# New duration estimates in the driver that orders a hybrid layer's instructions

## The chip, the cores and the metric

The kernel runs on one core of a Trainium2 chip. The core has a matrix engine (TensorE, PE in the profile), three engines for elementwise work (VectorE or DVE, ScalarE or ACT, GpSimd or POOL) and a queue that issues transfers (SyncE, SP); each of them works through its own instructions strictly in the order in which the program lists them. The metric is the time of one execution on the device in microseconds, as the median of several runs.

## What is computed

One layer of a generator over 1024 latent tokens and 256 context tokens of width 1024, in single precision:

```python
pl = project(modulate(x, sh_x, sc_x), w_in)        # 1024 latent tokens, 11 streams
pc = project(modulate(ctx, sh_c, sc_c), w_in)      # 256 context tokens
s_f = gla_final_state(kc, vc, la_fc)               # states after the context
s_b = gla_final_state(rev(kc), rev(vc), rev(la_bc))
o_gla = bidir_gla(q, k, v, la_f, la_b, s_f, s_b)   # 4 heads, both directions
a1 = softmax(q1 @ [ck1, k1].T / 8); a2 = softmax(q2 @ [ck2, k2].T / 8)
o_diff = (a1 - lam * a2) @ [cv, dv]                # 8 heads, 1024 queries, 1280 keys
a = rms_norm(o_gla) * gla_gain * silu(gla_gate)
b = rms_norm(o_diff) * diff_gain * (1 - lam_init) * silu(diff_gate)
y = sigmoid(m_gla) * (a @ w_br_gla) + sigmoid(m_diff) * (b @ w_br_diff)
x = x + g_x * (y @ w_out)
```

Before this a small product makes shifts, scales and gates from the conditioning. Queries and keys of the attention are normalised and rotated by position.

## The kernel before

Every large product is made of three matmuls on 128x128 weights and up to 512 columns (`mm3`): each operand is held as a high part `hi` in a faster format and a remainder `lo`, and the products hi·hi, hi·lo and lo·hi are added up. The split itself is work for ScalarE or GpSimd (the copy `hi`) and VectorE or GpSimd (the subtraction `lo`).

The work has these stages, in the order of the span:

- **Prologue** (`prologue`, `consts`, `consts_late`): inputs are loaded and normalised, the conditioning's product is made, the tokens are transposed into the tiles `h`.
- **Projections** (`stream` in `phase_a`): fifteen jobs, each 512 columns of the input projection for all tokens. Their results go to PSUM tiles `mm`, through ScalarE, VectorE and GpSimd, and out to memory. This stream has the lowest priority among the tasks, 9, and fills what time TensorE has left beside other tasks.
- **Linear attention** (GLA, `gla_head`): four heads one after another, from the eighth job of the stream on. A head loads its tensors (tile `gk` and others), makes running sums, transposes keys (tile `gt`), carries a state along ten chunks backward and forward (`upd`: a matmul on TensorE, then one VectorE instruction that adds it to the decayed state `gsb` or `gsf`), computes the products inside chunks (`intra`: differences and products on VectorE, exponentials on ScalarE) and combines them in the tile `go`. Its buffers are single or double.
- **Change of buffers**: when GLA is done, its pools are closed and the pools of attention's operands opened (`to_gla` sets `ev_b2`); then keys `kk`, values `vv` and queries `aq` are loaded. When the projections are done too, PSUM is handed over (`to_b` sets `ev_b`), and attention may begin.
- **Differential attention** (`att_scores`, `att_max`, `att_exp`, `att_mix`, `att_tr`, `att_split`, `att_av`, `att_fin`): 64 steps, one for each of 8 heads and 8 tiles of 128 queries. A step makes two sets of scores (PSUM tiles `st` and `s2`, the latter shown as `s` in the profile), takes maxima on VectorE and exponentials on ScalarE, combines the two softmaxes on VectorE, transposes the result on TensorE (PSUM tiles `b`), copies it on ScalarE (tile `ac`), splits it on GpSimd (tiles `at`), and multiplies it with the values. Every second step ends in a normalisation (`att_fin`, tiles `b1k`).
- **Fill** (`fill`): the rest of the projections (12 blocks of 128 columns) and the two branch products are cut into half tiles of 24 matmuls, which run at priority 9 beside attention in one PSUM bank (`mb`), and later in the banks `mc`. The number of half tiles that may have started is bound to the number of attention steps by `PACE = 1.3`.
- **End** (`phase_c`): the last branch products and the output projection.

What sets the order is the class `Driver`. While the program is being built, all stages run as Python generators, and the driver keeps a clock of its own: `now` for TensorE, and for each other engine the time `free` at which it has finished what it was given. Each emitted instruction goes through `Driver.op` with an estimated cost. It starts at the latest of its engine's free time and the times at which its operands are ready; it ends after its cost; and its result is ready `LAT` later (0.24 us for PE, 0.15 us for the others). A generator yields the time at which it wishes to go on, or an event; the driver takes the due generator of the best priority, and where none is due moves `now` forward. Generators that yield such a time are taken up to 1.0 us earlier (`AHEAD`), those that name an engine when that engine has at most 1.0 us of work left (`SLACK`). The estimates do not alter any instruction: they decide at which place of its engine's list, and of the transfer queue, each one stands. The chip then works through these lists, with waits where data aren't there yet.

The costs are set in `Engine.emit`, in `Hybrid.mm` (line 317 is the matmul), in `Hybrid.tr` (a transpose, line 329) and for transfers in `Driver.dma`. The profile attributes every elementwise instruction to line 185, every matmul to line 317 and every transpose to line 329, since these are helpers; tiles tell them apart.

Of the kernel before, what the change touches and what calls it, by code (L numbers as in the profile page):

```python
# [10 lines left out]
F32R = mybir.dt.float32r  # L11
# [45 lines left out]
class Driver:  # L57
# [58 lines left out]
        return At(end)  # L116

    def dma(self, nbytes, dst, src):
        t = max(self.free["DGE"], self.now, self.ready.get(self.key(src), 0.0)) + 0.6
        self.free["DGE"] = t  # L120
        t = max(self.free["DMA"], t + 0.6) + nbytes / 360e3
        self.free["DMA"] = t
        t += 1.8
        k = self.key(dst)
        self.ready[k] = max(t, self.ready.get(k, 0.0))
        return At(t)
# [48 lines left out]
class Engine:  # L175
# [5 lines left out]
    def __getattr__(self, what):  # L181
        f = getattr(self.eng, what)

        def emit(out, *args, **kw):
            f(out, *args, **kw)  # L185
            isap = lambda x: hasattr(x, "free_size")
            ins = [x for x in list(args) + list(kw.values()) if isap(x)]
            outs = [out] + [kw[k] for k in ("accum_out",) if k in kw]
            n = out.free_size()
            if what == "tensor_reduce":  # L190
                n = args[0].free_size()
            scalars = sum(1 for x in ins if x.free_size() == 1 and n > 1)
            psum = any(x.space == PSUM for x in ins)
            if self.name == "ACT":
                c = 0.06 + 0.000833 * n + 0.093 * scalars + (0.0 if psum else 0.04)
            elif self.name == "DVE":
                fast = what in ("tensor_scalar", "tensor_copy") and not psum
                c = 0.07 + n / 960 * (0.5 if fast else 2.0 if "scan" in what else 8.0 if what == "reciprocal" else 1.0)
            elif ALU.pow in args:
                c = 0.3 + 0.165 * n  # L200
            elif what == "tensor_tensor":
                c = 0.15 + 0.0021 * n
            else:
                c = 0.16 + 0.00083 * n + 0.083 * scalars
            return self.d.op(self.name, c, outs, ins)

        return emit
# [6 lines left out]
class Hybrid:  # L214
# [101 lines left out]
    def mm(self, out, lhsT, rhs, start, stop):  # L316
        self.nc.tensor.matmul(out, lhsT, rhs, start=start, stop=stop)  # L317
        n = rhs.free_size()
        c = (max(n, 256) if rhs.dtype == F32R else 2 * max(2 * n, 256)) / 2400
        return self.d.op("PE", c, [out], [lhsT, rhs])  # L320

    def mm3(self, out, sh, sl, mh, ml, first, last):
# [1588 lines left out]
```

## Time and profile before

| | |
|---|---|
| median of 3 runs | 1772.32 us (1772.30, 1772.32, 1776.98) |
| profiled execution | 1774.69 us, span 1773.0 us |
| instructions | 25057 |
| matmuls and transposes on TensorE | 8633, busy 96% of the span |
| VectorE, ScalarE, GpSimd busy | 60%, 43%, 41% |
| transfers | 260 MB, mean 147 GB/s |
| TensorE clock granted | 0.99 |

A matmul's duration in the profile runs from its start to a modelled end and overlaps with the next one; the distance from one start to the next is what a matmul costs in a sequence. In the timeline and in the chain, neighbouring instructions of one kind are merged into a row with their count ("x24"). A timeline row shows the start, the time taken, the engine, the line, the operation, the tile written and the tiles read, and in brackets the idle time ahead of it and what ended that. A row of the waits shows who waited for whom, the total in microseconds, the number of waits, and the longest. Times are counted from the start of the span.

### The profile page before, as it was taken

To read this page: it belongs to the slowest core of one execution; us is meant where nothing else is said; L and a number is where in the kernel's file an instruction comes from. 1 tells how busy PE (TensorE), PEld (TensorE's weight loads), DVE (VectorE), ACT (ScalarE), POOL (GpSimd) and SP (SyncE) were. 2 spreads that over 40 slices of the span, in tenths; PEclk is the share of its full clock that TensorE was granted. 3 is DMA by queue.
4 is the path that set the end of the run, shared out by engine and by line. 5 is a ranking of instruction groups with operands and counts; after the bars stand their busy time and mean duration, and the time that the engine had idled before them with its cause. 6 is when DMAs were issued, how large, how long until landed. Compare 5 with 4: busy or idle time off the path is not lost.

```text
span 1773.0 us, 25057 instructions
## 1 busy us (share of the span) xinstructions
PE 1703.7 (96%) x8633; PEld 1400.7 (79%) x8633; DVE 1057.8 (60%) x1895; ACT 761.9 (43%) x1759; POOL 735.6 (41%) x914
## 2 busy tenths in 40 slices
PE   8799999999999999999999999999999898999999
PEld 3688868888888888788788788788887787888887
DVE  4524332625564767878861987777877678525532
ACT  5536442212233444443442666666665555522200
POOL 1500000412323435545530477777876776731000
PEclk9899999999999999999999999999999999999999
DMA  7522452343653645546447245345447652268522
GB/s 275 174 88 101 154 173 89 108 142 122 182 181 117 190 141 144 178 137 176 137 134 193 71 121 145 96 125 128 116 114 234 184 150 93 81 200 301 185 101 84
DMA packets 245991, 259.97 MB, mean 147 GB/s; under 512 B 21948, under 2 KB 177508, under 8 KB 245864
## 3 DMA queue, kind: packets, MB, share of 16 engines
q1 hardware_dynamic: 245864, 258.37, 47.4%
q8 instruction: 68, 1.11, 0.3%
q14 instruction: 59, 0.48, 0.1%
HBM read 171.79 MB, written 86.52 MB: 146 GB/s over the span
## 4 chain that ended last, share of the span: by engine, by line
PE 77%; DVE 12%; DMA 3%; ACT 3%; issue 2%; POOL 1%; SPq 1%; ACTq 0%; DVEq 0%; POOLq 0%
PE mm L317 37%; PE mc L317 12%; PE mb L317 7%; DVE sm L185 6%; PE b L317 5%; PE s L317 4%; PE b L329 3%; PE go L317 2%; PE st L317 2%; PE tp L329 2%; PE gs L317 2%; PE gt L317 1%; DVE e L185 1%; DVE b1k L185 1%; DVE gd L185 1%
## 5 line engine op out<-in xcount | busy, mean ns | idle before, releaser
L317 PE MATMUL mm<-w,h 128*128 128x512 f32 x2304 | 570.5, 399 | 0.5 <-ACT w L185 0.3
L317 PEld LDWEIGHTS mm<-w,h 128*128 128x128 f32 x2304 | 425.7, 188 | 86.5 <-ACT w L185 0.7
L185 POOL TENSOR_TENSOR at<-ac,at 128x512 fp32r<-128x512 f32 (+1 forms) x192 | 237.6, 1237 | 16.0
L317 PE MATMUL mb<-h,wt 128*128 128x512 f32 x792 | 213.7, 406 | 5.5 <-DVE ft L185 5.3
L185 POOL TENSOR_SCALAR at<-ac 128x512 fp32r<-128x512 f32 (+1 forms) x192 | 136.4, 710 | 168.1 <-ACT ac L185 167.1
L185 POOL TENSOR_SCALAR sm<-sm 128x1 f32<-128x1 f32 (+1 forms) x78 | 18.6, 239 | 444.7 <-DVE sm L185 348.5
L185 DVE TENSOR_TENSOR w<-raw,w 128x512 fp32r<-128x512 f32 x136 | 97.8, 737 | 119.6 <-ACT w L185 117.3
L317 PEld LDWEIGHTS mb<-h,wt 128*128 128x128 f32 x792 | 140.1, 189 | 31.5 <-DVE ft L185 6.0
L185 ACT ACTIVATE p<-mm 128x512 f32<-128x512 f32 (+1 forms) x116 | 67.4, 588 | 218.1 <-PE mm L317 200.2
L185 ACT ACTIVATE ac<-b 128x512 f32<-128x512 f32 (+1 forms) x213 | 107.4, 511 | 122.2 <-PE b L329 102.6
L185 DVE TENSOR_REDUCE sm<-s 128x1 f32<-128x1024 f32 x128 | 155.6, 1216 | 2.8 <-PE s L317 1.6
L185 ACT ACTIVATE e<-s,sm 128x1024 f32<-128x1024 f32 x128 | 143.9, 1124 | 0.0
L317 PE MATMUL b<-at,vv 128*128 128x256 f32 x960 | 130.8, 290 | 9.6 <-ACT ac L185 7.1
L317 PE MATMUL mm<-h,w 128*128 128x512 f32 x576 | 138.6, 397 | 0.1
L317 PEld LDWEIGHTS b<-at,vv 128*128 128x128 f32 x960 | 123.4, 194 | 15.8 <-ACT ac L185 9.6
L317 PE MATMUL s<-kk,aq 128*128 128x512 f32 x512 | 132.7, 396 | 0.3 <-ACT p L185 0.3
L317 PEld LDWEIGHTS mm<-h,w 128*128 128x128 f32 x576 | 108.6, 191 | 24.8 <-DVE h L185 0.8
L185 POOL TENSOR_TENSOR sm<-sm,nhalf 128x1 f32<-128x1 f32 (+2 forms) x110 | 114.8, 1044 | 30.5 <-DVE sm L185 21.1
L185 DVE SCALAR_TENSOR_TENSOR e<-e,sm,e 128x1280 f32<-128x1280 f32 x64 | 103.8, 1622 | 0.1
L317 PEld LDWEIGHTS s<-kk,aq 128*128 128x128 f32 x512 | 90.9, 189 | 15.4 <-ACT p L185 0.5
L185 ACT ACTIVATE w<-raw 128x512 fp32r<-128x512 f32 x136 | 82.2, 626 | 40.3 <-PE mm L317 25.6
L329 PE MATMUL b<-ident,e 128*128 128x128 f32 x604 | 94.3, 278 | 5.0 <-ACT ac L185 4.5
(195 smaller groups left out, 2649.2 us busy)
## 6 DMA issues: line engine op xcount, KB each, us to landing
raw<-in_w_in SPq DMA_DIRECT2D x72, 512.0 KB, 4.6
aq<-d_qT SPq DMA_DIRECT2D x128, 128.0 KB, 4.1
d_kT<-pl SPq DMA_DIRECT2D x40, 256.0 KB, 2.3
d_dv<-pl SPq DMA_DIRECT2D x40, 256.0 KB, 2.3
gv<-d_v SPq DMA_DIRECT2D x40, 256.0 KB, 3.2
kk<-d_kT SPq DMA_DIRECT2D x32, 320.0 KB, 4.1
vv<-d_dv SPq DMA_DIRECT2D x16, 640.0 KB, 8.4
d_aT<-gpl SPq DMA_DIRECT2D x64, 128.0 KB, 1.9
```

Of the source, the lines that this page charges most:

```text
L185: f(out, *args, **kw)
L317: self.nc.tensor.matmul(out, lhsT, rhs, start=start, stop=stop)
L329: self.nc.tensor.transpose(out, src, self.ident[:n, :n])
```

## The change

Only the estimates change, in three places: transfers, elementwise instructions and matmuls. In the elementwise formulas n is the number of elements per partition; `scalars` counts operands of one element per partition (an accumulator output counted among them before), `psum` says that an input lies in PSUM, and `acc` that the instruction has an accumulator output.

```diff
     def dma(self, nbytes, dst, src):
-        t = max(self.free["DGE"], self.now, self.ready.get(self.key(src), 0.0)) + 0.6
+        t = max(self.free["DGE"], self.now, self.ready.get(self.key(src), 0.0)) + 0.45
         self.free["DGE"] = t
...
             scalars = sum(1 for x in ins if x.free_size() == 1 and n > 1)
             psum = any(x.space == PSUM for x in ins)
+            acc = "accum_out" in kw
+            scalars -= acc and n > 1
             if self.name == "ACT":
-                c = 0.06 + 0.000833 * n + 0.093 * scalars + (0.0 if psum else 0.04)
+                c = 0.2 + 0.000833 * n + 0.093 * scalars - (0.028 if psum else 0.0) + (0.21 if acc else 0.0)
             elif self.name == "DVE":
                 fast = what in ("tensor_scalar", "tensor_copy") and not psum
-                c = 0.07 + n / 960 * (0.5 if fast else 2.0 if "scan" in what else 8.0 if what == "reciprocal" else 1.0)
+                c = 0.16 + 0.055 * scalars + n * 0.00104 * (
+                    0.5 if fast else 2.0 if "scan" in what else 8.0 if what == "reciprocal" else 1.0)
             elif ALU.pow in args:
-                c = 0.3 + 0.165 * n
+                c = 0.4 + 0.155 * n
             elif what == "tensor_tensor":
-                c = 0.15 + 0.0021 * n
+                c = 0.18 + 0.00216 * n
             else:
-                c = 0.16 + 0.00083 * n + 0.083 * scalars
+                c = 0.19 + 0.00084 * n
             return self.d.op(self.name, c, outs, ins)
...
         self.nc.tensor.matmul(out, lhsT, rhs, start=start, stop=stop)
         n = rhs.free_size()
-        c = (max(n, 256) if rhs.dtype == F32R else 2 * max(2 * n, 256)) / 2400
+        c = 0.009 + max(n, 230) * 0.000428 if rhs.dtype == F32R else 0.006 + max(4 * n, 470) / 2400
         return self.d.op("PE", c, [out], [lhsT, rhs])
```

A transpose keeps its cost of 0.109 us, and `LAT`, `AHEAD`, `SLACK`, the priorities and `PACE` stay as they are.

## The prediction

> **What bounds the kernel now.** I read the page first, then busy time by stage, then the timelines of single engines, the chain and the waits. The page says that TensorE is the bound, so other engines matter only where they keep it waiting.
>
> ```profile
> span 1773.0 us, 25057 instructions
> PE 1703.7 (96%) x8633; PEld 1400.7 (79%) x8633; DVE 1057.8 (60%) x1895; ACT 761.9 (43%) x1759; POOL 735.6 (41%) x914
> PE 77%; DVE 12%; DMA 3%; ACT 3%; issue 2%; POOL 1%; SPq 1%; ACTq 0%; DVEq 0%; POOLq 0%
> ```
>
> The second view cuts the span where the work changes: prologue, projections alone, linear attention (GLA) beside projections, projections alone again, differential attention beside the fill, and the end. Its columns are width, then busy time with instruction counts per engine, clock, DMA share and GB/s.
>
> ```profile
> 0.00:90.00 90.00, 69.62 (x295) 42.12 (x296) 47.44 (x80) 47.96 (x87) 32.81 (x57) 0.91 0.65 223
> 90.00:480.00 390.00, 385.63 (x1769) 313.19 (x1768) 157.72 (x234) 136.51 (x210) 57.57 (x60) 1.00 0.39 125
> 480.00:936.00 456.00, 448.86 (x2204) 372.68 (x2204) 315.78 (x673) 182.91 (x475) 202.63 (x314) 1.00 0.51 155
> 936.00:968.50 32.50, 32.50 (x145) 26.90 (x144) 2.36 (x2) 5.16 (x8) 0.00 (x0) 1.00 0.97 235
> 968.50:1536.00 567.50, 535.24 (x3149) 454.51 (x3148) 443.83 (x772) 350.02 (x907) 404.76 (x442) 0.99 0.46 129
> 1536.00:1773.00 237.00, 231.86 (x1080) 191.32 (x1078) 90.63 (x135) 39.30 (x73) 37.80 (x42) 1.00 0.49 168
> ```
>
> TensorE is idle for 20.4 us in the prologue, 4.4 in the projections, 7.1 beside GLA, nothing from 936 to 968.5, 32.3 in attention and 5.1 at the end. The change adds and removes no instruction. It can only move work between these gaps, so attention's 32.3 us is the prize and the full stretch at 936 is what can be lost.
>
> **What the new figures say, against the trace.** The driver uses a cost for two things: when the engine is free again, and when the result is ready (the end plus LAT, 0.15 us, or 0.24 for PE). Here is ScalarE working without a gap.
>
> ```profile
> 1165.71 0.47 ACT L185 ACTIVATE e<-st,sm 128x256 f32<-128x256 f32 x1 [1.35 <-DVE sm L185]
> 1166.08 0.19 ACT L185 ACTIVATION_READ_ACCUMULATOR e<-st,sm 128x1 f32 x1
> 1166.17 1.11 ACT L185 ACTIVATE e<-s,sm 128x1024 f32<-128x1024 f32 x1
> 1167.17 0.20 ACT L185 ACTIVATION_READ_ACCUMULATOR e<-s,sm 128x1 f32 x1
> 1167.26 0.60 ACT L185 ACTIVATE ac<-b 128x512 f32<-128x512 f32 x1
> 1167.74 0.60 ACT L185 ACTIVATE ft<-mb 128x512 f32<-128x512 f32 x1
> ```
>
> From start to start the small exponential takes 0.46 us, the large one 1.09, the copy 0.48. The old formula gives 0.459, 1.099 and 0.4865: it is the distance between starts. The new one gives 0.688, 1.328 and 0.5985, which is the duration shown (0.60 for the copy) or the sum of an instruction's and its accumulator read's durations. VectorE shows the same.
>
> ```profile
> 1165.93 1.54 DVE L185 SCALAR_TENSOR_TENSOR e<-e,sm,e 128x1280 f32<-128x1280 f32 x1
> 1167.39 0.15 DVE L185 SCALAR_TENSOR_TENSOR sm<-sm,sm 128x2 f32<-128x2 f32 x1
> 1170.19 0.69 DVE L185 TENSOR_REDUCE sm<-st 128x2 f32<-128x512 f32 x1 [1.01 <-PE st L317]
> 1170.80 0.15 DVE L185 TENSOR_REDUCE sm<-sm 128x2 f32<-128x4 f32 x1
> ```
>
> Distances are 1.46 and 0.61, durations 1.54 and 0.69. The old figures are 1.403 and 0.603, the new 1.546 and 0.692. So the new costs take an engine as occupied for its whole latency, and LAT is then added to that: a copy's result was due 0.4865 + 0.15 = 0.64 us after its start, which is about right for a 0.60 us instruction, and is now due at 0.75. GpSimd hardly moves: the 512-wide subtraction goes from 1.225 to 1.286, against 1.337 here.
>
> ```profile
> L185 POOL TENSOR_TENSOR at<-ac,at 128x512 fp32r<-128x512 f32 x128 | 171.1, 1337 | 10.7
> 326.82 5.49 PE mm L317 x24
> ```
>
> TensorE goes the other way. The chain's piece of 24 matmuls takes 5.49 / 24 = 0.229 us each; the driver believed 512 / 2400 = 0.213 and will believe 0.228. So far its PE clock ran 7% fast, which gave every other engine 7% less time per matmul than it has: a margin that was hidden there. The new PE figure takes that margin away and the new ACT and DVE figures put a larger one in its place.
>
> The Trainium skill (Perfetto Trace Analysis, "Optimizing Scalar/DVE Operations") says that a ScalarE or VectorE instruction's profiled latency holds about twice the access overhead for which the engine is busy, because the write acknowledgement overlaps with the next instruction. The rows above agree (0.60 shown, 0.48 apart). By that rule the new occupancies are too long and the old ones right, and it speaks against this half of the change.
>
> **Linear attention: price of the longer estimates.** In this stage the driver puts as many projection matmuls (three at a time, 3 x 0.213 = 0.64 us, new 0.684) between two steps of GLA as it thinks the step takes. One step of the state recurrence is here:
>
> ```profile
> 650.28 0.59 PE L317 MATMUL gt<-gv,gkt 128*128 128x256 f32 x2
> 650.52 1.73 PE L317 MATMUL mm<-w,h 128*128 128x512 f32 x6
> 650.91 0.48 DVE L185 SCALAR_TENSOR_TENSOR gsb<-gsb,gsm,gt 128x256 f32<-128x256 f32 x1 [0.59 <-PE gt L317]
> ```
>
> After the state matmul the driver waited 0.24 + 0.337 + 0.15 = 0.727 us, and will wait 0.24 + 0.481 + 0.15 = 0.871. In units of three matmuls that is 1.14, then 1.27: 12% more. The key transposes' copy (0.273 to 0.385) goes from 1.04 to 1.13 units, 9% more. In the intra-chunk step (two 128-wide subtractions, an exponential, a product, 0.15 after each) it is 1.51 to 1.88 us, or 2.35 to 2.74 units, 16% more. About 12% more projection work is thus asked for between GLA steps. Not all of it comes: a wait of 1.14 or 1.27 units is two units either way, as the six matmuls of the row show, and GLA's own matmuls do not stretch. The bounds are 0 (all rounded away) and 12%; I take the middle, 6%.
>
> GLA runs from the first head's load at 480 to its last transposes at 934.4:
>
> ```profile
> 479.98 0.50 SPq L282 DMA_DIRECT2D gk<-d_k  x1
> 934.37 0.38 PE L329 MATMUL tp<-ident,gp 128*128 128x128 f32 x2
> 934.50 34.31 PE L317 MATMUL mm<-h,w 128*128 128x512 f32 x150
> 937.25 3.72 SPq L282 DMA_DIRECT2D kk<-d_kT  x6
> 941.01 8.26 SPq L282 DMA_DIRECT2D vv<-d_dv  x3
> 949.32 6.71 SPq L282 DMA_DIRECT2D aq<-d_qT  x8
> aq<-d_qT SPq DMA_DIRECT2D x128, 128.0 KB, 4.1
> 968.65 0.64 PE L317 MATMUL st<-kk,aq 128*128 128x256 f32 x4
> ```
>
> So 6% of 454 us is 27 us. What hides it is the block of 150 projection matmuls that is left when GLA ends, 34.2 us. But that block already hides something: keys, values and queries of attention are loaded only once GLA's buffers are closed, and go through one queue. The first pair's four query transfers are issued by about 949.32 + 6.71 / 2 = 952.7 and land 4.1 later, at 956.8, which is 22 us after GLA's end. Only 968.65 - 956.8 = 12 us are spare. Total projection work is fixed, so GLA may end 12 us later for nothing; every further microsecond leaves TensorE with neither projections nor loaded queries. Price: 27 - 12 = +15 us; bounds 0 and 54 - 12 = +42.
>
> **Attention: what it may give.** The waits there are for results that the driver thought ready:
>
> ```profile
> PE b L329 <- DVE b1k L185: 8.7, 10, 3.9
> PE b L317 <- ACT ac L185: 7.1, 5, 1.7
> PE mb L317 <- DVE ft L185: 5.3, 3, 2.9
> PE b L329 <- ACT ac L185: 4.5, 6, 1.9
> ```
>
> They are transposes and products placed too early behind ACT and DVE work. Longer estimates place them later, with fill matmuls before them. The ACT waits (11.6 us) are the ones whose estimate grows most (copy and LAT per 512-wide matmul: 0.6365 / 0.213 = 2.99, then 0.7485 / 0.228 = 3.28, 10% more). The products also wait for GpSimd's splitting, which in the same measure becomes shorter (1.375 / 0.213 = 6.46, then 1.436 / 0.228 = 6.30), so I count only half of the ACT waits and no other: -6 us. Bounds: 0, and -20 if nearly two thirds of the 32.3 us go. Should fewer fill matmuls be left afterwards, the end stage, idle for 5 us now, loses its cover; that is a rival below.
>
> **DMA and prologue.** The issue figure of 0.6 us becomes 0.45; the rows above have 0.50 for one key load and 0.84 for a query load. The estimate shifts issue by tenths, so I take 0. The prologue holds one long wait of a transpose for VectorE, which any reordering may lengthen or remove; bounds -10 and +10, taken as 0 since nothing in the formulas points either way.
>
> ```profile
> PE gt L329 <- DVE p L185: 10.7, 2, 10.1
> ```
>
> **Sum.** The profiled execution took 1774.69 us (span 1773.0 and 1.7 around it), 2.4 above the median of the three runs (1772.32; 1772.30 to 1776.98). 1774.7 + 15 - 6 + 0 = 1783.7; as a median 1783.7 - 2.4, about 1781.
>
> **The rivals.** (1) Attention gains and GLA stays under its cover. This ends faster. It decides where GLA's stretch is under 12 us, 2.7% of 454, so where whole units of three matmuls swallow most of the 12%. For it: the six-matmul row, and GLA's stage is nearly free of waits as it is. Against it: the intra-chunk step is longer than two units and has room to grow. Time: -10 of attention's 32.3 us (the ACT waits almost whole), 1772.3 - 10 = 1762; with the bound of -20, 1752.
> (2) The fill runs out. Attention has 64 query tiles and may use 40 half tiles of fill of 24 matmuls; these rows show how many ran there.
>
> ```profile
> L317 PE MATMUL mb<-h,wt 128*128 128x512 f32 x792 | 213.7, 406 | 5.5 <-DVE ft L185 5.3
> ```
>
> That is 792 / 24 = 33, so seven are left. If longer estimates open wider gaps, a rate over 40 / 33 = 1.21 times as high empties them early. A query tile without fill still needs VectorE's 443.83 / 64 = 6.9 us, against TensorE's own (535.24 - 33 x 24 x 0.229) / 64 = 5.5: 1.4 us idle each, 17 us for the last twelve. 1772.3 + 17 = 1789. Against it: a copy's wait grows by only 10%.
> (3) The order hardly changes or gains and losses cancel: 1772.
>
> **Chances and range.** Forecast (GLA outlasts its spare cover) 0.42; rival 1 0.36; rival 2 0.10; rival 3 0.12. Faster 0.36, same 0.12, slower 0.52, taking 0.3% or 5 us as the least that a measurement of this kernel tells from no change. Both signs are likely. The forecast's own range is 1775 to 1808, from GLA's +42 less attention's 6 at the top to a stretch just beyond its cover at the bottom. The range that holds 8 in 10 reaches down through most of rival 1: 1754 to 1808.
>
> **What would show it.** In the profile after, GLA's last transposes should come at about 960 instead of 934, the block of pure projection matmuls behind them should shrink from 150 to under 60, and the first score matmul should stand at about 983 with TensorE idle ahead of it, released by DMA `aq`. Attention's idle time should fall from 32 to about 26 us, with the waits on ACT `ac` shorter. Wrong: GLA ends before 947 and the first scores stay at 968; then the time is set by attention alone, and faster if its idle time falls below 27. Wrong too: `mb` matmuls well over 960, which means the fill ran out, or a change of over 5 us before 90 us.

## The result and the profile after

The change makes no difference that can be told: 1776.12 us median (1770.69 to 1778.61, 14 runs) against 1775.09 us before (14 runs); ratio 1.0003, 95% interval 0.9994 to 1.0012. The profiled execution took 1776.08 us with a span of 1774.4, 1.4 us over the span of before.

Under this equal sum the stages moved. These are the same cuts of busy time as before the change (width, then PE, PEld, DVE, ACT, POOL, clock, DMA share, GB/s).

```profile
0.00:90.00 90.00, 69.84 (x286) 41.67 (x287) 46.89 (x80) 48.20 (x87) 32.68 (x57) 0.91 0.63 220
480.00:936.00 456.00, 455.66 (x2239) 381.86 (x2239) 304.03 (x666) 181.43 (x470) 192.98 (x307) 1.00 0.50 156
936.00:968.50 32.50, 25.31 (x119) 20.77 (x118) 4.44 (x9) 7.04 (x15) 2.52 (x8) 0.94 0.64 159
968.50:1536.00 567.50, 533.24 (x3165) 456.38 (x3166) 438.12 (x773) 351.25 (x907) 397.15 (x446) 0.98 0.47 133
```

Beside linear attention TensorE's idle time fell from 7.1 us to 0.3. From 936 to 968.5, where it had none, it has 7.2. The timeline of TensorE after the change shows that hole, and the transfer queue's shows what fills it.

```profile
950.67 0.38 PE L332 MATMUL tp<-ident,gp 128*128 128x128 f32 x2
950.80 10.51 PE L320 MATMUL mm<-h,w 128*128 128x512 f32 x45
973.85 1.51 PE L320 MATMUL st<-kk,aq 128*128 128x256 f32 x4 [12.54 <-DMA aq<-d_qT]
```

```profile
481.38 0.51 SPq L285 DMA_DIRECT2D gk<-d_k  x1
952.45 3.71 SPq L285 DMA_DIRECT2D kk<-d_kT  x6
956.20 9.29 SPq L285 DMA_DIRECT2D vv<-d_dv  x3
965.54 7.73 SPq L285 DMA_DIRECT2D aq<-d_qT  x8
```

Linear attention runs from 481.38 to 950.67, 469.3 us instead of 454.4. 45 projection matmuls are left behind it instead of 150. They are done at 961.3, and TensorE waits 12.54 us for the queries, which stand in the queue behind six key loads and three value loads. The first scores come at 973.85 instead of 968.65, only 5.2 us later, because TensorE had lost less time beside linear attention.

The price of the wait does not end with it. These are the first eight large score matmuls, before and after the change, and the stretch after the change in which the latter ran.

```profile
969.55 2.11 PE L317 MATMUL s<-kk,aq 128*128 128x512 f32 x8 [0.26 <-ACT p L185]
975.16 3.37 PE L320 MATMUL s<-kk,aq 128*128 128x512 f32 x8
973.85:978.10 4.25, 4.25 (x11) 3.38 (x12) 1.68 (x2) 0.00 (x0) 0.00 (x0) 0.50 0.86 253
```

The granted clock fell to 0.50 during the wait, at 964.5, and stayed there until 978.1. So the first 4.25 us of attention ran at half speed, which is worth about 2 us (an estimate: half of 4.25). TensorE counts as busy in such a stretch, so the busy share does not show the loss.

From the first scores to the end of the span it takes 800.5 us instead of 804.4, though single profiles of one order differ by as much: the fourth experiment below has the order of before in attention (two of TensorE's 4224 instructions stand at other places) and takes 800.4. What TensorE waits for in the attention window has changed its kind:

```profile
PE b L332 <- ACT ac L185: 12.8, 15, 1.4
PE st L320 <- DMA aq<-d_qT: 12.5, 1, 12.5
PE b L332 <- DVE b1k L185: 10.1, 15, 1.4
PE b L320 <- ACT ac L185: 3.1, 3, 1.0
```

The products' waits for the copies `ac` fell from 7.1 us to 3.1, and the fill's waits for `ft` from 5.5 us (5.3 of them on VectorE) to 0.7; the transposes' waits for `ac` rose from 4.5 us to 12.8.

### The profile page after: what moved, and what is told of

Same layout as the page of the kernel before. It is cut to its first block, busy times and chain, and to the rows that moved or that the text cites. A ratio compares the mean times of both kernels' runs of the same rounds, so it can differ in the third digit from the quotient of the medians.

```text
span 1774.4 us, 25140 instructions
## 1 busy us (share of the span) xinstructions
PE 1700.1 (96%) x8633; PEld 1403.5 (79%) x8633; DVE 1037.6 (58%) x1895; ACT 762.2 (43%) x1759; POOL 716.2 (40%) x914
## 4 chain that ended last, share of the span: by engine, by line
PE 86%; DVE 4%; DMA 3%; POOL 2%; ACT 2%; issue 2%; SPq 1%; ACTq 0%; POOLq 0%; DVEq 0%
PE mm L320 40%; PE mc L320 12%; PE mb L320 8%; PE b L320 6%; PE s L320 5%; PE b L332 3%; PE go L320 3%; DVE sm L185 2%; POOL at L185 2%; PE gs L320 2%; PE gt L320 2%; PE st L320 2%; PE tp L332 2%; SPq L285 1%; DMA w<-in_w_ada 1%
## 5 line engine op out<-in xcount | busy, mean ns | idle before, releaser
L185 POOL TENSOR_TENSOR at<-ac,at 128x512 fp32r<-128x512 f32 (+1 forms) x192 | 221.9, 1156 | 16.0
L320 PE MATMUL mb<-h,wt 128*128 128x512 f32 x792 | 219.9, 407 | 1.2 <-ACT ft L185 0.7
L185 POOL TENSOR_SCALAR at<-ac 128x512 fp32r<-128x512 f32 (+1 forms) x192 | 145.2, 756 | 158.7 <-ACT ac L185 149.3
L320 PE MATMUL mm<-h,w 128*128 128x512 f32 x576 | 144.4, 403 | 2.0 <-DVE h L185 1.5
L320 PE MATMUL s<-kk,aq 128*128 128x512 f32 x512 | 137.7, 404 | 0.0
L332 PE MATMUL b<-ident,e 128*128 128x128 f32 x604 | 94.1, 275 | 23.5 <-ACT ac L185 12.8
L185 POOL TENSOR_TENSOR sm<-sm,nhalf 128x1 f32<-128x1 f32 (+2 forms) x110 | 108.2, 983 | 13.7 <-DVE sm L185 7.2
L332 PEld LDWEIGHTS b<-ident,e 128*128 128x128 f32 x604 | 71.7, 140 | 44.7 <-ACT ac L185 18.6
L185 ACT ACTIVATE e<-st,sm 128x256 f32<-128x256 f32 x128 | 60.7, 474 | 99.8 <-DVE sm L185 83.6
```

The costliest lines, as they stand in the source:

```text
L332: self.nc.tensor.transpose(out, src, self.ident[:n, :n])
```

## Experiments

Ratios are to the kernel before, run beside each on the same chip, with 95% intervals. A thousandth is 1.8 us.

**1. The matmul estimate alone.**

```diff
-        c = (max(n, 256) if rhs.dtype == F32R else 2 * max(2 * n, 256)) / 2400
+        c = 0.009 + max(n, 230) * 0.000428 if rhs.dtype == F32R else 0.006 + max(4 * n, 470) / 2400
```

> Only the matmul estimate is the new one (0.213 to 0.228 us for 512 columns); elementwise and transfer estimates are the old ones. Theory (the hidden margin of 7% is taken away, nothing is put in its place): linear attention ends earlier, with some 246 projection matmuls left behind its last transposes instead of 150, so at about 934 - 96 x 0.229 = 912 us; the query loads stay hidden; TensorE waits more often beside linear attention and in attention (its idle time there above 35 us instead of 32), and the time is 3 to 12 us longer than before. Rival (the true rate of TensorE is the useful part): idle time falls in attention and the time is 3 us or more shorter than before.

Measured: 1803.99 us, ratio 1.0173 (1.0156 to 1.0189), about 30 us slower, far more than expected. TensorE's timeline around the end of linear attention, then the queue's:

```profile
917.11 0.38 PE L329 MATMUL tp<-ident,gp 128*128 128x128 f32 x2
945.55 41.79 PE L317 MATMUL mm<-h,w 128*128 128x512 f32 x174 [11.68 <-ACT w L185]
987.18 0.64 PE L317 MATMUL st<-kk,aq 128*128 128x256 f32 x4
```

```profile
922.03 3.05 SPq L282 DMA_DIRECT2D kk<-d_kT  x5
925.12 7.30 SPq L282 DMA_DIRECT2D vv<-d_dv  x3
932.47 7.93 SPq L282 DMA_DIRECT2D aq<-d_qT  x8
940.50 1.04 SPq L282 DMA_DIRECT2D raw<-in_w_in  x2
```

Linear attention ends 17 us early, as the theory has it, but this brings a loss that it did not foresee: attention's loads now enter the queue ahead of the last weights (`raw`) that the projections need, and TensorE waits 11.68 us for these. The first scores stand at 987.18, 18.5 us late; from there to the end it takes 816.0 us, 11.7 more than before. The truer rate of TensorE, by itself, is harmful.

**2. The elementwise estimates alone** (the matmul line of the diff above and the 0.45 of the transfers taken back).

> Only the elementwise estimates are new; matmul and transfer estimates are the old ones. Theory: the longer estimates alone stretch linear attention; some 33 projection matmuls are left behind it instead of 150 (45 with the whole change), so it ends near 954 us, TensorE waits for DMA aq for about 12 us or more ahead of the first scores, which stand at 974 to 980; the stage beside linear attention has no idle time; the time is within 6 us of before. Rival (the matmul estimate causes the later end of linear attention): its last transposes stay at about 934 and there is no wait for aq.

Measured: 1799.24 us, ratio 1.0140 (1.0122 to 1.0157). What was expected ahead of attention came (33 matmuls left, a wait for the queries, though the stage beside linear attention still has 5.7 us of idle time); the time did not.

```profile
959.66 0.38 PE L332 MATMUL tp<-ident,gp 128*128 128x128 f32 x2
959.79 7.79 PE L320 MATMUL mm<-h,w 128*128 128x512 f32 x33
981.06 0.77 PE L320 MATMUL st<-kk,aq 128*128 128x256 f32 x2 [13.48 <-DMA aq<-d_qT]
```

```profile
PE b L332 <- ACT ac L185: 23.3, 23, 2.2
```

Linear attention ends 25 us late and the first scores 12.4 us late. In attention the transposes wait 23.3 us for `ac`, against 4.5 before, but other waits are shorter: from the first scores on TensorE is idle for 38.7 us in all, against 37.4. What is longer there is its time at half the clock, 25.8 us against 13.7 (the last section says what goes ahead of such stretches). The profiled execution is the fastest of the four (1793.02), so it shows somewhat less than the median's loss. Each half of the change loses over 20 us, and the two together nothing. For the end of linear attention the record shows that the halves pull in opposite directions (917 with one, 960 with the other, 951 with both, 934 with neither); for attention's order this is not shown.

**3. The changed kernel with the values loaded after the first queries.**

```diff
     def att_values(self):
         yield self.ev_b2
+        yield self.ev_q[0, 0]
```

> The changed kernel, with one line more: the values of attention are loaded only after the first pair's queries, so that those don't stand behind three value loads in the transfer queue (9.3 us of issue there). Theory (the gain is lost to the uncovered query load): the wait for DMA aq of 12.5 us ahead of the first scores shrinks to 2 to 5 us, the first score matmul moves from 974 to 964 - 967, and the time falls by 6 to 11 us below the changed kernel, so to about 0.995 of the kernel before. Rival (keys or the hand-over of PSUM are as late): the first score stays within 3 us of 974 and the time is the same.

Measured: 1769.03 us, ratio 0.9978 (0.9969 to 0.9987).

```profile
956.25 8.21 SPq L285 DMA_DIRECT2D aq<-d_qT  x8
965.69 4.50 SPq L285 DMA_DIRECT2D vv<-d_dv  x3
```

```profile
965.14 0.77 PE L320 MATMUL st<-kk,aq 128*128 128x256 f32 x2 [4.67 <-DMA aq<-d_qT]
```

The query loads follow the keys at once, the wait falls from 12.54 us to 4.67, and the first scores come 8.7 us earlier. Against the changed kernel that is 1.0003 - 0.9978 = 0.0025, about 4 us: less than the 6 to 11 us expected, but the two intervals do not meet. That the query load is uncovered, and that the value loads ahead of it in the queue are the cause, is shown by the wait. How much of the 4 us comes from it is not, because the line also changed attention's order: 2757 of TensorE's 4224 instructions from the first scores on stand at other places than in the changed kernel.

**4. The same line in the kernel before.**

> The kernel before, with the same line (values after the first queries). Theory: its query loads are covered by 150 projection matmuls anyway, the first score stays at 968 to 969, and the time is that of before within 2 us. Rival (an earlier query helps by itself, or later values hurt): the time differs from before by over 4 us.

Measured: 1774.35 us, ratio 0.9997 (0.9984 to 1.0009); the first scores stand at 969.6. As expected: under 150 projection matmuls the loads' order is free.

**5. The matmul estimate, and everything else in proportion.**

```diff
-    LAT = dict(PE=0.24, ACT=0.15, DVE=0.15, POOL=0.15)
+    LAT = dict(PE=0.2568, ACT=0.1605, DVE=0.1605, POOL=0.1605)
...
-            return self.d.op(self.name, c, outs, ins)
+            return self.d.op(self.name, 1.07 * c, outs, ins)
...
-        c = (max(n, 256) if rhs.dtype == F32R else 2 * max(2 * n, 256)) / 2400
+        c = 0.009 + max(n, 230) * 0.000428 if rhs.dtype == F32R else 0.006 + max(4 * n, 470) / 2400
```

> The new matmul estimate, with every old elementwise estimate and LAT multiplied by 1.07 (transposes, transfers, AHEAD and SLACK as before). Theory (only the ratio between TensorE and the other engines counts, and the old too fast TensorE was a margin of 7%): with the ratio put back the order is about the old one; some 135 projection matmuls are left behind linear attention (150 before, 246 with the matmul estimate alone), the first scores stand at 968 to 971, and the time is within 6 us of before. Rival (the truer matmul estimate is harmful in itself): still 15 us or more slower.

Measured: 1788.72 us, ratio 1.0091 (1.0076 to 1.0107). Half of the theory holds.

```profile
935.12 0.38 PE L329 MATMUL tp<-ident,gp 128*128 128x128 f32 x2
935.25 30.91 PE L317 MATMUL mm<-h,w 128*128 128x512 f32 x135
966.00 0.64 PE L317 MATMUL st<-kk,aq 128*128 128x256 f32 x4
```

```profile
968.50:1536.00 567.50, 527.74 (x3094) 447.28 (x3093) 436.24 (x763) 347.33 (x898) 399.09 (x437) 0.98 0.43 126
```

Linear attention is back where it was (935.12, 135 matmuls behind it, the first scores even 2.7 us earlier), so there the ratio does decide. Attention isn't: by 1536 TensorE has done 3094 matmuls and transposes, against 3149 before, though it began earlier. It is idle for 39.8 us in the window, against 32.3, and the granted clock is lower (0.98 against 0.99). Either what was not scaled matters (transposes, `AHEAD`, `SLACK`, transfers), or attention's order turns on small shifts. This run can't tell which; the last four bear on it.

**6. The new estimates in attention only.** A flag that is set with `ev_b` chooses between both sets.

```diff
             d.set(self.ev_b)
+            d.new = True
...
+            if self.d.new:
...
+            else:
...
```

> The old estimates until attention may begin, the new ones from there on. Theory (the change gains some 4 us in attention and after it, and loses 5 us ahead of it): the first scores stay at 968 to 970, from there to the end it takes 800 us instead of 804, and the time is 2 to 6 us below before. Rival (the gain after the first scores in the changed kernel is only what its later start brought, since loads were further by then): the time is within 1.5 us of before.

Measured: 1767.05 us, ratio 0.9969 (0.9956 to 0.9981), 5.5 us faster. The first scores stand at 969.1. The attention window and its waits (the helper lines have moved by the added lines):

```profile
968.50:1536.00 567.50, 540.39 (x3216) 461.17 (x3215) 436.37 (x779) 355.60 (x919) 406.98 (x457) 0.99 0.45 130
```

```profile
PE b L350 <- ACT ac L186: 13.9, 19, 1.5
PE b L350 <- DVE b1k L186: 5.7, 15, 1.3
PE b L335 <- ACT ac L186: 3.1, 3, 1.0
```

27.1 us idle instead of 32.3. TensorE's order is that of before up to the first scores and that of the changed kernel from there on, without exception in tiles and shapes; in the next experiment it is the other way round.

**7. The new estimates ahead of attention only** (the same flag, the other way round).

> The new estimates until attention may begin, the old ones from there on. Theory: the wait for aq of 12 us is there as in the changed kernel, the first scores stand at 973 to 975, from there to the end it takes 804 us as before, and the time is 3 to 7 us above before. Rival (the wait is made up for later whatever the estimates): within 2 us of before.

Measured: 1775.06 us, ratio 1.0021 (1.0010 to 1.0031), 3.7 us slower.

```profile
971.52 1.58 PE L335 MATMUL st<-kk,aq 128*128 128x256 f32 x4 [12.33 <-DMA aq<-d_qT]
```

The wait of 12.33 us is there with the old estimates in attention. The first scores stand about 2 us earlier than in the changed kernel, although the order up to there is the same; that much is scatter between two profiles. With the sixth experiment this splits the result: +3.7 us ahead of attention (1.8 to 5.5), -5.5 in it and behind it (-7.8 to -3.4), -1.8 as a sum, against the whole change's +0.5 (-1.1 to +2.1). Within these intervals the two parts add up to the whole.

**8. The first experiment with late values** (the edits of 1 and 3 together).

> The matmul estimate alone as in the first experiment, with the values loaded only after the first queries. In that experiment linear attention ended early, and TensorE waited 11.7 us for the projections' last weights, whose load stood behind fourteen loads of attention in the transfer queue. Theory (that queue is the price): the value loads (7.3 us of issue) no longer stand ahead of the weights, the wait for ACT w falls to 4 to 6 us, and the time falls by 5 to 10 us, to 1.008 to 1.014 of before. Rival (the loss is in attention's order alone): the time stays at 1.017.

Measured: 1797.81 us, ratio 1.0141 (1.0127 to 1.0155). TensorE's wait for the projections' last weights in this kernel:

```profile
PE mm L317 <- ACT w L185: 4.8, 1, 4.8
```

4.8 us instead of 11.68, and about 6 us of time come back. The order on TensorE is that of the first experiment but for two instructions, so the weights' wait is shown to come from the queue. (In the first experiment seventeen loads of keys, values and queries stood ahead of these weights; the expectation counts fourteen.) The larger part of the first experiment's loss is elsewhere: from the first scores on, this profile takes 817.9 us against 804.4. Why attention's order is worse there stays open.

**9 to 12. Is attention's gain more than chance?** From the start of attention on, all elementwise costs are multiplied by 0.98 or 1.02, once with the new set there (on top of experiment 6) and once with the old.

```diff
-            return self.d.op(self.name, c, outs, ins)
+            return self.d.op(self.name, (0.98 if self.d.new else 1.0) * c, outs, ins)
```

> Old estimates until attention, the new ones from there on, with the elementwise costs there multiplied by 0.98 (the change itself raises them by 9 to 50%). Theory A (the new estimates make a better order in attention): the time stays 2 to 9 us below before (0.995 to 0.999), as with the factor 1. Theory B (any small shift of an estimate makes another order, good or bad by chance): it moves by over 5 us from the 0.997 of the factor 1, or comes above 1.000.

> The same with the factor 1.02. Theory A: 0.995 to 0.999 of before. Theory B: over 5 us from 0.997, or above 1.000.

> The kernel before, with the old elementwise costs multiplied by 0.98 from the start of attention on. Theory A: within 4 us of before (0.998 to 1.002), and above both kernels with the new estimates. Theory B: it moves by over 5 us either way, and may lie below them.

> The same with the factor 1.02. Theory A: within 4 us of before, and above both kernels with the new estimates. Theory B: it moves by over 5 us either way, and may lie below them.

| set in attention | x 0.98 | x 1 | x 1.02 |
|---|---|---|---|
| new | 0.9901 (0.9886 to 0.9916), 1757.02 us | 0.9969 (0.9956 to 0.9981), 1767.05 us | 0.9984 (0.9974 to 0.9994), 1771.73 us |
| old | 1.0034 (1.0022 to 1.0046), 1781.01 us | 1 | 1.0019 (1.0009 to 1.0029), 1778.25 us |

The attention windows of the new set with 0.98 and 1.02, then of the old with 0.98 and 1.02:

```profile
968.50:1536.00 567.50, 548.13 (x3279) 466.85 (x3278) 451.77 (x784) 360.32 (x930) 432.58 (x468) 0.99 0.46 130
```

```profile
968.50:1536.00 567.50, 538.18 (x3208) 459.20 (x3207) 442.07 (x779) 355.42 (x917) 414.92 (x454) 0.99 0.46 129
```

```profile
968.50:1536.00 567.50, 533.96 (x3145) 452.74 (x3144) 447.47 (x774) 353.72 (x908) 404.46 (x444) 0.99 0.46 128
```

```profile
968.50:1536.00 567.50, 532.57 (x3126) 452.61 (x3125) 435.37 (x766) 348.32 (x897) 386.53 (x436) 0.98 0.46 127
```

TensorE's idle time is 19.4 and 29.3 us with the new set (27.1 at factor 1), 33.5 and 34.9 with the old (32.3 at 1). Neither theory is right alone. A shift of 2% moved the new set by -12 and +3 us and the old by +6 and +3, so an order is to a good part luck. But all three times with the new set lie below all three with the old: the means, 0.9951 and 1.0018, are 12 us apart, with standard deviations of 8 and 3 us within the sets. By chance alone three and three fall so once in twenty, and the middle pair is the one that raised the question. The gain in attention is perhaps more than luck; its size of 5.5 us in one pair says little, and 1757.02 us is the best of a few draws rather than the work of the factor 0.98. It is the fastest kernel of this study.

How an order becomes time can be added up. The table has, for these six profiles, the time from the first scores to the end of the span, TensorE's idle time in it, and the time that TensorE worked while the granted clock was 0.50.

| order in attention | to the end | idle | at half clock | to the end, less idle, less half of the half-clock time |
|---|---|---|---|---|
| new x 0.98 | 786.1 | 24.5 | 6.8 | 758.2 |
| new x 1 | 796.2 | 32.8 | 6.7 | 760.0 |
| new x 1.02 | 797.6 | 34.6 | 9.0 | 758.5 |
| old x 1 | 804.4 | 37.4 | 13.7 | 760.1 |
| old x 1.02 | 809.3 | 41.0 | 19.3 | 758.7 |
| old x 0.98 | 815.1 | 44.7 | 20.6 | 760.1 |

What remains is nearly the same in all six, so the orders differ by waits and by the half-clock stretches that go with them. About a quarter of the 29 us between the first row and the last is the clock.

## Why the prediction was right or wrong

**Direction and size.** Forecast was a slowdown to 1781 us within 1754 to 1808, from two opposing terms, +15 ahead of attention and -6 in it. Both terms exist and have the signs that were given. They are closer in size than forecast, so they cancel, which had been given a chance of 0.12. The forecast's 9 us of slowdown did not come. That 1776.12 us lies well inside the range is owed to its width of 54 us, made to hold most of a rival too. The 2.4 us taken off for the median came from three runs; with fourteen the median of before is 1775.09, level with the profile.

**The estimates' meaning: right.** The old elementwise figures are the distance between starts, the new ones the duration; the old matmul figure hid a margin of 7%. Experiments 1 and 2 show that the two edits move the end of linear attention in opposite directions (each about 25 to 30 us slower alone), and 5 that with the ratio put back it ends where it did (935.12 against 934.37). In attention it doesn't suffice, which the prediction had not foreseen.

**Linear attention's stretch: the mis-sized step.** It was taken as 6% or 27 us, the middle between 0 and 12%. It measured 469.3 - 454.4 = 14.9 us, 3.3%. The 6% was a choice between bounds; which of the longer waits were rounded away is not shown. The mechanism came as described, to the named releaser: 45 matmuls behind it where "under 60" was written, and a wait of 12.54 us on `aq`. The spare cover was put at 12 us; the way from the end of linear attention to the first scores measured 973.85 - 950.67 = 23.2 us instead of the 22.4 reckoned, so 11.1 us were spare. Later end (16.3 us, with its later start) less spare gives the 5.2 us by which the first scores moved, in place of 15. What the prediction had no term for is the half clock behind the wait, some 2 us. Experiment 7 puts the price of the part ahead at 3.7 us (1.8 to 5.5), inside the bounds of 0 and 42 and near the lower one.

**Attention's gain: right in size by luck, wrong in its waits.** -6 was written, as half of the 11.6 us that TensorE waited for `ac`; -5.5 (-7.8 to -3.4) was measured in experiment 6. But those waits did not shrink. In experiment 6 they are 17.0 us: the products' did fall (7.1 to 3.1), and the transposes' rose (4.5 to 13.9). What fell were the waits for `b1k` (11.8 to 5.7 over all lines) and the fill's for `ft` (5.5 to 0.7), and the work at half clock (13.7 to 6.7 us). The named step failed, so the agreement in size is luck; the same estimates 2% shorter gain 17.6 us. In the changed kernel itself, attention's idle time in the window, without the wait for the queries, is 28.9 us where about 26 was written.

**Prologue and transfers.** Idle time before 90 us is 20.2 us against 20.4, as the 0 had it, with other waits in the place of the long one, and linear attention starts 1.4 us later. The transfer figure alone was not tried.

**The rivals.** The first (faster, linear attention under its cover) decided at a stretch of 12 us; with 14.9 it was missed by little, and experiment 6 is this rival with the stretch taken away: faster, by less than the 10 us given, and not through the `ac` waits on which that figure rested. The second (the fill runs out) didn't happen: the page shows 792 `mb` matmuls again. The third, gains and losses that cancel, is what happened. That a stretch the other way would cost as much, through weights queued behind attention's loads, was named by none of them; experiment 1 found it.

## What to carry to other kernels

For a driver that orders instructions by estimates, a truer figure is not by itself a better order: the truer matmul figure alone cost 30 us here, and the longer elementwise figures alone (true as durations, too long as distances between starts) cost 25. In linear attention that is because the old errors had been balanced against each other; in attention the cause stays open. Try a set of estimates together with its near neighbours, because a shift of 2% moved this kernel by up to 12 us and one pair of runs can't tell a better model from a lucky order. And where one stage's filler also hides the next stage's loads, look at the order in the transfer queue: one line that put the queries ahead of the values brought the first scores 8.7 us forward, and the time fell by about 4 us.

## What the runs showed of the hardware

**Waits of about half of 3.4 us cost more than themselves.** In all fourteen traces the recorded clock of TensorE is either 1.00 or 0.50, and it stays at 0.50 for 3.4 us or a multiple of that, unless the run ends. Between the first scores and the last 30 us of the spans, 50 such stretches began. In the 3.41 us ahead of each of them TensorE was idle for at least 1.48 us, ahead of 47 for at least 1.7. Of 3072 pieces of 3.41 us there that were followed by full clock, none had more than 1.89 us of idle time and only eleven had 1.7 or more. Where TensorE is busy in the half-clock stretch, up to 1.7 us are lost (half of 3.4). Two waits on `ac` of 1.75 us each in the kernel before had this price:

```profile
1147.67 3.11 PE L317 MATMUL b<-at,vv 128*128 128x256 f32 x18 [1.75 <-ACT ac L185]
1149.10:1152.50 3.40, 3.40 (x18) 3.40 (x17) 0.00 (x0) 2.37 (x6) 2.08 (x4) 0.50 0.40 138
1291.06 3.13 PE L317 MATMUL b<-at,vv 128*128 128x256 f32 x18 [1.75 <-ACT ac L185]
1292.40:1295.80 3.40, 3.40 (x18) 3.40 (x18) 0.00 (x0) 2.46 (x6) 2.11 (x3) 0.50 0.41 143
```

So the sum of the waits is not their price: it also matters how many of them are long or stand close together.

**The issue of one kind of load takes different times.** The same three value loads took 8.26 us of issue in the kernel before and 9.29 in the changed one, both ahead of the queries, 7.30 in experiment 1, and 4.50 behind the queries in experiment 3. Why is not shown. An instruction behind them waits for that, so a load's place in the queue costs more than its own count of instructions suggests.
